# A hybrid decoder block: convolution's carry summed on GpSimd, gates' input sums in one stage, unread work dropped, stages in another order

## The chip, the cores and the metric

The kernel runs on one core of one Trainium2 chip, as one program. The time is in device microseconds (us) of that core; three runs of the kernel before gave 2437.46, 2438.08 and 2443.91 us, median 2438.08. The engines are called as in the profile: PE is TensorE (matmuls; PEld its weight loads), DVE VectorE, ACT ScalarE, POOL GpSimd, SP SyncE, which issues most DMAs. Each engine takes its instructions in the order in which they were given to it, and an instruction that waits holds those behind it.

## What is computed

One decoder block over 2048 tokens of width 1024, all in float32. A norm, then one projection for two groups of heads: four of a gated delta rule (GDN) with a causal convolution of width 4 over the tokens on q, k and v, and four of retention; their outputs go through gates, an output projection and a residual sum; then a second norm, an MLP with a convolution of width 3 and a gate, a residual sum and a last norm. Cut to what matters here:

```python
def reference(x, ...):
    n = _rms_norm(x, attn_norm_w)
    (gq, gk, gv, gg, ga, gb, rq, rk, rv, rg) = split(n @ w_in)
    mix = concat([_gated_deltanet(gq, gk, gv, gg, ga, gb, ...), _retention(rq, rk, rv, rg)])
    h = x + mix @ w_out
    h = h + _conv_glu_mlp(_rms_norm(h, mlp_norm_w), mlp_w_up, mlp_conv_w, mlp_w_down)
    return _rms_norm(h, final_norm_w)

# gated delta rule: q, k, v = silu(causal_conv4(.)); per chunk of tokens
t_mat = triangular_solve(eye + m, eye)          # m strictly lower, from k, beta and decay
def step(state, inp):                           # chunk after chunk
    u = u_b - w_c @ state
    o = qd_c @ state + qk_c @ u
    state = state * cd_c + kd_c.T @ u
    return state, o                             # first state: zeros; last state: not used
# retention: the same form, r = r * chunk_gamma + kv_c, first r: zeros, last r: not used
```

## The kernel before

**Tiling.** The tokens are cut into four blocks of 512 (NB = 4, TB = 512), a block into four chunks of 128 (NT = 4). Each float32 operand of a large matmul is split into a high and a low part (ScalarE copies the high part, VectorE subtracts), and each product is made as three matmul passes (`mm3`, lines 118 to 120; 539 to 541 for the token-major projections). The projections for the gates, the output projection (`W`) and both MLP products use a scheme with seven products in place of eight; their inputs are sums of quarters of the norm's output and of the weights. The MLP comes after the four blocks: `mlp_up` (line 1115) and `mlp_down` (line 1314).

**Stages.** `mixers` makes for each block a table of items: `pro` norm; `k0`, `q0`, `kq`, `v0` retention projections; `a`, `c`, `f`, `e`, `d` the GDN's projections with the convolution and what follows; `b0`, `b1` the triangular solve for the heads' first and second pair; `l0`, `l1` its upper levels; `r00` to `r13` the recurrence (pair, chunk); `h`, `y` retention; `g`, `G` gated outputs; `O`, `Q` weight sums for the seven-product schemes; `S` and `T` the sums of the norm's input for gate products 6, 7 and 5, 3; `P` and `p` gate products; `W` output projection; `N` second norm; `U` steps of MLP-up. The string `ORDER` lists the items of all blocks in the order in which they are written; the digit behind `U` says nothing, each takes the next step. From this a scheduler with a model of the engines' times makes the order of each engine's instructions, and buffers are given out from rings whose sizes are in `BUFS`.

**The convolution** (`conv`, line 404) works on a tile of 128 channels and 512 tokens: ScalarE scales the last tap, VectorE adds the shifted other taps (line 408). The first three tokens also need the three tokens before the block: `halo` keeps these, VectorE multiplies and adds them (line 412, 1, 2 and 3 columns) and copies the block's last three into it (line 414).

**The solve** (`gdn_base`, the part of `b0`, `b1`): its input goes through DRAM (written from ScalarE's queue, read into `Nb`, line 772), GpSimd makes 62 dependent steps (lines 781 and 783, alternating; the printed shape shrinks from 31 to 1 columns), the result is written to DRAM (line 786), read back as `AT` (line 794), and VectorE transposes it to `NT` (line 796).

**The recurrence** (`gdn_rec`, line 846), for a pair of heads and a chunk: TensorE `ks` (860, state times k and q), VectorE `kv` (863), TensorE `wps` (870), VectorE `u` (873, printed as `pers`), TensorE `sps` (878), VectorE state (880) and output (883). The next chunk's `ks` needs the state.

**Retention** (`ret_head`, `ret_out`): TensorE `rr` (964) makes each chunk's share of the state, `ro` (992, 993) the output from the chunk itself and from the state.

**Gates' sums** (`combos`, line 455): for each of two stages the four loads of `xT` (462), ScalarE's scaling (465), three or four VectorE sums (468), the split.

**The last norm** (`final`, line 1347): sum of the two halves' squares, scaling and epsilon (1350), power on GpSimd (1351), then the two halves of the output on ScalarE and VectorE.

## Time and profile before

| | |
|---|---|
| runs | 2437.46, 2438.08, 2443.91 us |
| profiled execution: span from first to last instruction | 2432.2 us |
| profiled execution: its own time beside the span | not listed; the median run is 5.9 us above the span |
| instructions | 35992 |
| TensorE busy | 2383.1 us (98%) |
| VectorE / ScalarE / GpSimd busy | 1658.6 / 1073.5 / 422.5 us |
| DMA | 652.40 MB, mean 268 GB/s |

In the rows a matmul's name is out<-in. `x2` behind a row of the timeline stands for instructions in a row of one kind; the bracket gives the engine's idle time before and what ended it. The stretches give for each engine the busy time within a part of the span, and the clock that was granted to TensorE as a share of full speed. A float32 matmul of 128x128 on 128x128 appears as two rows, a pass of the split products as one.

### The profile page before, as it was taken

Reading aid. Unit: us, or ns where it says so; the run is one execution under the profiler, and the core shown is the slowest. Engines: PE = TensorE matmul, PEld = TensorE weight load, DVE = VectorE, ACT = ScalarE, POOL = GpSimd, SP = SyncE. Lnnn points to the kernel's source line nnn. Section 1 sums busy time; section 2 is a strip of 40 time slices with the busy share of each in tenths; the row PEclk is TensorE's granted clock in tenths of the full one; section 3 lists DMA queues with packets and bytes.
Section 4 is the critical chain, followed back from the end, with each engine's and each line's share of the span. In section 5 each row is a group of like instructions: output and inputs, shape, how many; then the busy total and the mean of one; then the engine's idle time right before and its main releaser. Section 6 shows DMA issues by size and latency. Waiting matters only on the chain.

```text
span 2432.2 us, 35992 instructions
## 1 busy us (share of the span) xinstructions
PE 2383.1 (98%) x12404; PEld 2004.0 (82%) x12404; DVE 1658.6 (68%) x3187; ACT 1073.5 (44%) x2286; POOL 422.5 (17%) x753
## 2 busy tenths in 40 slices
PE   8999899999999999999999999999999999999998
PEld 8888788888887888887788888888888888888887
DVE  6965786574744872778889888995556676554684
ACT  6744555555444652466543434432222233432341
POOL 2154113510043003130000100000000002431030
PEclk9999999999999999999999999999999999999999
DMA  9955789986767874697898878767768588764782
GB/s 333 381 194 186 304 305 365 318 317 242 286 238 251 307 253 156 227 344 292 325 357 315 305 284 315 291 241 255 250 230 313 198 276 275 262 215 148 224 249 103
DMA packets 307142, 652.40 MB, mean 268 GB/s; under 512 B 51024, under 2 KB 130320, under 8 KB 306960
## 3 DMA queue, kind: packets, MB, share of 16 engines
q1 hardware_dynamic: 290240, 635.80, 73.8%
q10 hardware_dynamic: 16720, 14.30, 1.9%
q8 instruction: 98, 1.61, 0.3%
q14 instruction: 84, 0.69, 0.1%
HBM read 444.12 MB, written 205.88 MB: 267 GB/s over the span
## 4 chain that ended last, share of the span: by engine, by line
PE 52%; DVE 1%; issue 0%; ACT 0%; DMA 0%; POOLq 0%; POOL 0%; ACTq 0%
PE p L118 11%; PE p L120 11%; PE p L119 11%; PE d L120 6%; PE d L119 6%; PE d L118 6%; PE p L1215 1%; PE p L1214 1%; PE p L1213 1%; PE wo L118 0%; PE wo L120 0%; PE wo L119 0%; DMA wv<-kW 0%; DVE st L1146 0%; DVE x L1125 0%
## 5 line engine op out<-in xcount | busy, mean ns | idle before, releaser
L119 PE MATMUL p<-x,wu 128*128 128x512 f32 x1176 | 457.5, 389 | 0.7 <-DVE x L1125 0.5
L118 PE MATMUL p<-x,wu 128*128 128x512 f32 x1176 | 452.7, 389 | 0.0
L120 PE MATMUL p<-x,wu 128*128 128x512 f32 x1176 | 450.1, 389 | 0.0
L119 PEld LDWEIGHTS p<-x,wu 128*128 128x128 f32 x1176 | 220.8, 188 | 47.3 <-DVE x L1125 1.5
L118 PEld LDWEIGHTS p<-x,wu 128*128 128x128 f32 x1176 | 220.7, 188 | 46.0 <-ACT x L1124 0.3
L120 PEld LDWEIGHTS p<-x,wu 128*128 128x128 f32 x1176 | 220.7, 188 | 45.7
L1253 DVE SCALAR_TENSOR_TENSOR acc<-uc,base,acc 128x1022 f32<-128x1022 f32 (+1 forms) x176 | 220.8, 1278 | 37.4 <-ACT acc L1250 37.2
L1206 DVE TENSOR_TENSOR uc<-p,uc 128x512 f32<-128x512 f32 x224 | 153.0, 686 | 134.3 <-PE p L120 130.0
L539 PE MATMUL tok<-wc,n 128*128 128x512 f32 (+2 forms) x576 | 196.4, 351 | 7.7 <-ACT n L449 5.3
L540 PE MATMUL tok<-wc,n 128*128 128x512 f32 (+2 forms) x576 | 199.4, 348 | 0.0
L541 PE MATMUL tok<-wc,n 128*128 128x512 f32 (+2 forms) x576 | 195.9, 348 | 1.3 <-DVE n L452 1.3
L184 POOL TENSOR_TENSOR vt<-vr 128x512 f32<-128x512 f32 x44 | 71.9, 1634 | 639.0 <-DMA vr<-in_w_d 440.7
L118 PE MATMUL d<-v,uu 128*128 128x512 f32 x448 | 174.3, 389 | 0.0
L119 PE MATMUL d<-v,uu 128*128 128x512 f32 x448 | 174.3, 389 | 0.0
L120 PE MATMUL d<-v,uu 128*128 128x512 f32 x448 | 174.3, 389 | 0.0
L118 PE MATMUL chm<-n,wc 128*128 128x512 f32 x384 | 152.5, 397 | 1.8 <-ACT og L583 1.8
L119 PE MATMUL chm<-n,wc 128*128 128x512 f32 x384 | 151.6, 395 | 0.0
L120 PE MATMUL chm<-n,wc 128*128 128x512 f32 x384 | 151.3, 394 | 0.0
L1250 ACT ACTIVATE acc<-uc,base 128x1024 f32<-128x1024 f32 x88 | 97.1, 1144 | 92.9 <-DVE uc L1206 46.3
L539 PEld LDWEIGHTS tok<-wc,n 128*128 128x128 f32 x576 | 109.9, 192 | 21.1 <-ACT n L449 5.3
L408 DVE SCALAR_TENSOR_TENSOR ca<-ca,base 128x511 f32<-128x511 f32 (+2 forms) x144 | 109.5, 760 | 21.4 <-ACT ca L405 20.8
L540 PEld LDWEIGHTS tok<-wc,n 128*128 128x128 f32 x576 | 110.0, 191 | 12.3 <-DVE wc L208 0.2
(280 smaller groups left out, 5047.9 us busy)
## 6 DMA issues: line engine op xcount, KB each, us to landing
wu<-wu SPq DMA_DIRECT2D x308, 512.0 KB, 5.7
wc<-wd SPq DMA_DIRECT2D x116, 512.0 KB, 5.2
wv<-kW SPq DMA_DIRECT2D x112, 512.0 KB, 6.7
wc<-kP SPq DMA_DIRECT2D x84, 512.0 KB, 6.2
ur<-au SPq DMA_DIRECT2D x56, 512.0 KB, 5.1
wd<-wc SPq DMA_DIRECT2D x44, 512.0 KB, 7.3
wur<-in_w_u SPq DMA_DIRECT2D x44, 512.0 KB, 6.1
au<-st SPq DMA_DIRECT2D x88, 256.0 KB, 5.5
```

Of the source, the lines that this page charges most:

```text
L118: PE.matmul(ps, ah, bh, start=(first and i == 0), stop=False, skip_group_check=chk)
L119: PE.matmul(ps, ah, bl, start=False, stop=False, skip_group_check=chk)
L120: PE.matmul(ps, al, bh, start=False, stop=(i == n - 1), skip_group_check=chk)
L184: POOL.tensor_tensor(tt[:, j], a, b_, op=ALU.subtract)
L408: DVE.scalar_tensor_tensor(acc[:, s:], ps[:, :TB - s], w, acc[:, s:], op0=ALU.mult, op1=ALU.add)
L539: PE.matmul(ps, ah, wh, start=(k == 0), stop=False)
L540: PE.matmul(ps, ah, wl, start=False, stop=False)
L541: PE.matmul(ps, al_, wh, start=False, stop=(k == KT - 1))
L1206: add = lambda o, ps, a: DVE.tensor_tensor(o, ps, a, op=ALU.add)
L1213: PE.matmul(ps[i], wh, xh, start=(kt == 0), stop=False)
L1250: ACT.activation(acc, u, AF.Copy, scale=mcw[:, ci, 2:3])
L1253: DVE.scalar_tensor_tensor(acc[:, t:], u[:, :T2 - t], w, acc[:, t:], op0=ALU.mult, op1=ALU.add)
```

## The change

1. **Convolution.** What the next block needs of the last three tokens is multiplied and summed ahead, on GpSimd (three multiplications and two additions on 1 to 3 columns), not in the last block. In the next block VectorE adds the three columns in one instruction.
2. **Gates' sums.** `T` is gone; `S` makes the sums for products 6, 7, 5 and 3 from one load of each `xT` part and one scaling, with four sums instead of three and four.
3. **Unread work.** In the first chunk of block 0 the state is zero: `ks` and what reads it is left out there, the state is copied instead of updated, and the states are no longer set to zero. In the last chunk of block 3 the state's update is left out, with the scaled keys, `rr` and the retention state that only it needs.
4. **Last norm.** In the last output tile the second half's sum of squares is scaled at product 5, the first half's square is scaled as it is made, and one instruction between them and the power is gone.
5. **Order and buffers.** `ORDER` and some sizes in `BUFS` are new.

```diff
-BUFS = {... "NT": 6, "AT": 10, "o": 6, ... "wsq": 5, ... "sc": 15, ... "Nb": 6, ... "rrow": 5}
+BUFS = {... "NT": 8, "AT": 11, "o": 7, ... "wsq": 6, ... "sc": 14, ... "Nb": 7, ... "rrow": 4}
-ORDER = ("... 0r10 0r11 0p0 1pro 0O3 0h2 0Q0 0r12 0y2 0p1 0g0 1k0 0r13 0h3 ... 1S 1kq 1P1 1h2 1y2 1l1 1r03 1h3 1P4 1T 1P6 ..."
-         "... 3r11 3r12 3y3 2W4 2N 3g1 3W1 3r13 3W2 3G1 3W6 3W7 3W5 U1 U2 U3 U4 3W4 3W3 U9 U0 U6 U7 U8 U5 3N U10")
+ORDER = ("... 0r10 0r11 0r12 0p0 0p1 0O3 0h2 0Q0 0y2 0r13 1pro 0g0 0h3 1k0 ... 1S 1kq 1P1 1h2 1y2 1l1 1r03 1h3 1P4 1P6 ..."
+         "... 3r11 2W4 3y3 3r12 2N 3r13 3g1 3W1 U0 U9 3W2 3G1 3W6 U1 3W7 U2 U3 U4 3W5 U8 3W4 3W3 U6 U7 3N U10 U5")
...
-    for t in Sst + Rst:
-        POOL.memset(t, 0.0)
...
-        if not first:
-            for s in range(1, ntap):
-                w = wt[:, ntap - 1 - s:ntap - s]
-                DVE.scalar_tensor_tensor(acc[:, :s], halo[:, ntap - 1 - s:], w, acc[:, :s],
-                                         op0=ALU.mult, op1=ALU.add)
-        DVE.tensor_copy(halo, ps[:, TB - (ntap - 1):])
+            DVE.tensor_tensor(acc[:, :ntap - 1], acc[:, :ntap - 1], halo, op=ALU.add)
+        if not last:
+            POOL.tensor_scalar(halo, ps[:, TB - (ntap - 1):], wt[:, :1], None, op0=ALU.mult)
+            for s in range(1, ntap - 1):
+                tmp = small("ht", 2, 4)[:, :s]
+                POOL.tensor_scalar(tmp, ps[:, TB - s:], wt[:, ntap - 1 - s:ntap - s], None, op0=ALU.mult)
+                POOL.tensor_tensor(halo[:, :s], halo[:, :s], tmp, op=ALU.add)
...
-                    j = int(5 not in ids)
-                    tt(j, ALU.add, a21, a22)
-                    if 6 in ids:
-                        tt(0, ALU.subtract, tm[:, j], a11)
-                        tt(1, ALU.subtract, a11, a21)
-                    else:
-                        tt(1, ALU.subtract, a12, a22)
-                        tt(2, ALU.subtract, a11, a21)
-                        tt(1, ALU.add, tm[:, 1], tm[:, 2])
+                tt(1, ALU.subtract, a11, a21)
+                tt(2, ALU.add, a21, a22)
+                tt(0, ALU.subtract, tm[:, 2], a11)
+                tt(3, ALU.subtract, a12, tm[:, 0])
+                for j, ids in ((0, (6, 7)), (2, (5, 3))):
...
-                for c in range(NT):
+                for c in range(NT - (b == NB - 1)):
                     ACT.activation(kd[:, c * P:(c + 1) * P], ps[:, c * P:(c + 1) * P], AF.Copy,
...
+                fresh, ending = b == 0 and c == 0, b == NB - 1 and c == NT - 1
+                if not fresh:
+                    ps = rbank("ks")
...
+                        if k or not ending:
+                            PE.matmul(ps[:, (k * n + i) * P:(k * n + i + 1) * P], e[w][:, sl],
+                                      u[:, i * P:(i + 1) * P], start=True, stop=True)
...
+                    if fresh:
+                        DVE.tensor_copy(Sst[h], pn)
+                    elif not ending:
...
             if tp == 7:
+                ss = sst[t1][:, 1:]
+                DVE.tensor_scalar(ss, ss, 1.0 / D, EPS, op0=ALU.mult, op1=ALU.add)
                 DVE.tensor_tensor(c22, c22, fnw[:, TB:], op=ALU.mult)
...
-            square(t1, 0)
-            final(t1, n == len(steps) - 1)
+            last = n == len(steps) - 1
+            square(t1, 0, D ** -0.5 if last else 1.0)
+            final(t1, last)
```

**What moves, on VectorE, block 0's second pair.** Three places of the order follow. The first is VectorE around the transpose of block 0's second solve (`AT` to `NT`, line 796), where block 1's norm (`n1`) and its weights' split (`wc`) are being made; `kv` and `pers5` are the recurrence of the first pair. Before:

```order
L863 SCALAR_TENSOR_TENSOR kv_893<-ks_1825,pers4_547,kv_893 128x128
L863 SCALAR_TENSOR_TENSOR kv_1070<-ks_1825,pers4_547,kv_1070 128x128
L796 STREAM_TRANSPOSE NT_1286<-AT_1285 128x512
L452 SCALAR_TENSOR_TENSOR n1_2525<-xk_2520,base_60,n1_2525 128x512
L452 SCALAR_TENSOR_TENSOR n1_2530<-xk_2528,base_60,n1_2530 128x512
L356 TENSOR_TENSOR wc_2484<-wraw_2485,wc_2484 128x264
L356 TENSOR_TENSOR wc_2491<-wraw_2485,wc_2491 128x264
L796 STREAM_TRANSPOSE NT_1575<-AT_1574 128x512
L452 SCALAR_TENSOR_TENSOR n1_2533<-xk_2528,base_60,n1_2533 128x512
L356 TENSOR_TENSOR wc_2496<-wraw_2497,wc_2496 128x264
L873 TENSOR_TENSOR pers5_1309<-wps_1834,pers4_547 128x256
```

After (the same transpose is now line 790, the state's update 883, the output 889, a weight sum 295, the gated output 572, `kv` 859):

```order
L883 SCALAR_TENSOR_TENSOR pers2_124<-pers2_124,pers4_405,sps_1858 128x128 x2
L889 TENSOR_TENSOR o_1830<-sps_1858,o_1830 128x2x128
L452 SCALAR_TENSOR_TENSOR n1_2864<-xk_2862,base_60,n1_2864 128x512
L354 TENSOR_TENSOR wc_2534<-wraw_2528,wc_2534 128x264
L452 SCALAR_TENSOR_TENSOR n1_2867<-xk_2862,base_60,n1_2867 128x512
L902 SCALAR_TENSOR_TENSOR pers4_405<-pers4_405,pers5_1333 128x4
L295 TENSOR_TENSOR wg_2716<-wvt_2693,wg_2716 128x512
L572 SCALAR_TENSOR_TENSOR mix_2407<-o_1830,pers5_1333,mix_2407 128x128 x4
L295 TENSOR_TENSOR wg_2721<-wvt_2694,wg_2721 128x512
L790 STREAM_TRANSPOSE NT_1310<-AT_1309 128x512
L354 TENSOR_TENSOR wc_2539<-wraw_2540,wc_2539 128x264
L859 SCALAR_TENSOR_TENSOR kv_814<-ks_1881,pers4_405,kv_814 128x128
```

The transpose stood between `kv` and `pers5` of one chunk; now that chunk's state and output are made ahead of it.

**On GpSimd, block 2's first solve.** A row of the solve's two alternating steps (`Nb` is its input, `pers4` its result so far), before:

```order
L781 TENSOR_TENSOR pers4_547<-Nb_7557,pers4_547 128x3x22
L783 TENSOR_TENSOR pers4_547<-pers4_547 128x3x22
L781 TENSOR_TENSOR pers4_547<-Nb_7557,pers4_547 128x3x21
L783 TENSOR_TENSOR pers4_547<-pers4_547 128x3x21
L781 TENSOR_TENSOR pers4_547<-Nb_7557,pers4_547 128x3x20
L783 TENSOR_TENSOR pers4_547<-pers4_547 128x3x20
```

After (the steps are lines 775 and 777; lines 410 to 414 are the convolution's carry, `ca` its input):

```order
L775 TENSOR_TENSOR pers4_405<-Nb_7589,pers4_405 128x3x21
L410 TENSOR_SCALAR pers1_117<-ca_7521,base_60 128x3
L777 TENSOR_TENSOR pers4_405<-pers4_405 128x3x21
L414 TENSOR_TENSOR pers1_117<-pers1_117,pers3_225 128x1
L775 TENSOR_TENSOR pers4_405<-Nb_7589,pers4_405 128x3x20
L414 TENSOR_TENSOR pers1_117<-pers1_117,pers3_225 128x2
L777 TENSOR_TENSOR pers4_405<-pers4_405 128x3x20
```

The carry's steps stand within the solve; 15 of them in this solve.

**On TensorE, the last recurrence of block 3's second pair** (`ks`, `wps`, `sps` as above; `pers_1309` and `pers_1333` are `u`). Before:

```order
L870 MATMUL wps<-kv,AT 128x128 x2
L878 MATMUL sps<-pers_1309,kv 128x128 x2
L878 MATMUL sps<-pers_1309,AT 128x128 x2
L860 MATMUL ks<-pers_124,ykq 128x128 x4
L870 MATMUL wps<-kv,AT 128x128 x2
```

After (`p` are MLP-up products with their input `x` and weights `wu`, `nps` transposes of block 2's second norm):

```order
L856 MATMUL ks<-pers_124,ykq 128x128 x4
L118 MATMUL p_12346<-x_0_11939,wu 128x512
L119 MATMUL p_12346<-x_0_11939,wu 128x512
L120 MATMUL p_12346<-x_0_11939,wu 128x512
L1115 MATMUL nps<-base,Cw 128x128 x4
L867 MATMUL wps<-kv,AT 128x128 x2
L118 MATMUL p_12468<-x_0_11942,wu 128x512
L119 MATMUL p_12468<-x_0_11942,wu 128x512
L120 MATMUL p_12468<-x_0_11942,wu 128x512
L876 MATMUL sps<-pers_1333,kv 128x128 x2
```

Products of MLP-up and transposes now stand between the steps of one chunk.

More of the change, by code (lines that the diff above doesn't have):

```diff
@@ L955, in rstep @@
         def rstep(h, Rc, rr, c, dst):
+            if b == 0 and c == 0:
+                DVE.tensor_copy(dst, rr[:, :P])
+                return
             DVE.scalar_tensor_tensor(dst, Rc[c], float(gamma[h] ** 128), rr[:, c * P:(c + 1) * P], op0=ALU.mult, op1=ALU.add)
@@ L961, in f @@
                 rr = rbank("rr")
-                for c in range(NT):
+                for c in range(NT - (b == NB - 1)):
                     sl = slice(c * P, (c + 1) * P)
```

102 lines of the change are left out of this document (54 added, 48 removed), and 22 rows, old and new, of the table ORDER.

## The prediction

> **What bounds the kernel now.** I read the page's busy shares first, then the stretches of the span, then what TensorE waited for and the timelines around the long waits.
>
> ```profile
> span 2432.2 us, 35992 instructions
> PE 2383.1 (98%) x12404; PEld 2004.0 (82%) x12404; DVE 1658.6 (68%) x3187; ACT 1073.5 (44%) x2286; POOL 422.5 (17%) x753
> ```
>
> TensorE (PE) is busy for 98% of the span, so an engine that is only made less busy gives nothing. The time can fall in two ways: fewer matmuls, or fewer of the pauses of TensorE. This execution has a span of 2432.2 us; the three runs have a median of 2438.08, 5.9 us more. I make the sum against the span and add 5.9 at the end. The stretches (length, then busy time and count for each engine, granted clock, DMA share, GB/s) tell where the pauses are:
>
> ```profile
> core 0: us, PE busy (x) PEld busy (x) DVE busy (x) ACT busy (x) POOL busy (x), PEclk, DMA share, GB/s
> 0.00:180.00 180.00, 172.71 (x938) 148.18 (x939) 133.92 (x293) 110.49 (x281) 55.65 (x106) 1.00 0.82 303
> 180.00:300.00 120.00, 108.47 (x780) 94.31 (x779) 73.55 (x196) 61.98 (x155) 37.44 (x76) 0.96 0.68 243
> 520.00:540.00 20.00, 16.62 (x167) 13.50 (x166) 15.94 (x39) 10.88 (x20) 0.00 (x0) 0.83 0.84 323
> 720.00:800.00 80.00, 74.67 (x590) 62.90 (x589) 38.78 (x115) 36.55 (x104) 27.76 (x85) 1.00 0.77 259
> 1080.00:1130.00 50.00, 42.56 (x351) 36.64 (x350) 38.54 (x102) 36.23 (x95) 5.14 (x6) 0.97 0.69 244
> 1180.00:2416.00 1236.00, 1236.00 (x5470) 1023.84 (x5470) 878.47 (x1210) 448.50 (x659) 134.31 (x116) 1.00 0.75 260
> 2416.00:2432.20 16.20, 9.04 (x40) 7.13 (x38) 4.04 (x8) 2.17 (x5) 1.08 (x2) 0.91 0.17 65
> ```
>
> From 1180 to 2416 TensorE has no idle time at all and the full clock: there only fewer matmuls would help, and the change takes none away. The idle time is length less busy: 11.5 us where block 0's recurrence meets block 1's projections (180 to 300), 3.4 around 530, 5.3 at block 2's solve (720 to 800), 7.4 in the last recurrence (1080 to 1130). The clock adds to it: 0.96 of full speed over 120 us loses about 4.8 us, 0.97 over 50 us about 1.5.
>
> The largest pause is at 218 us:
>
> ```profile
> 209.54 0.61 DVE L863 SCALAR_TENSOR_TENSOR kv<-ks,pers,kv 128x128 f32<-128x128 f32 x2 [0.88 <-PE ks L860]
> 218.19 0.71 DVE L796 STREAM_TRANSPOSE NT<-AT 128x512 f32<-128x512 f32 x1 [8.04 <-DMA AT<-z]
> 222.40 0.42 DVE L873 TENSOR_TENSOR pers<-wps,pers 128x256 f32<-128x256 f32 x1
> ```
>
> ```profile
> 219.59 0.39 PE L541 MATMUL tok<-wc,n 128*128 128x264 f32 x1 [1.26 <-DVE n L452]
> 222.87 1.23 PE L878 MATMUL sps<-pers,kv 128*128 128x128 f32 x4 [2.89 <-DVE pers L873]
> ```
>
> ```profile
> 210.00:218.00 8.00, 8.00 (x43) 6.86 (x42) 0.15 (x1) 2.28 (x8) 1.92 (x3) 1.00 0.56 131
> 218.00:230.00 12.00, 7.84 (x69) 6.83 (x68) 10.07 (x22) 6.45 (x16) 1.02 (x1) 0.72 0.98 333
> 524.70:531.60 6.90, 5.71 (x70) 4.58 (x70) 5.90 (x15) 2.22 (x6) 0.00 (x0) 0.51 1.03 411
> ```
>
> VectorE (DVE) issues in order. It stands 8.04 us before a transpose whose input comes back from the solve through DRAM; queued behind it are the norm's `n`, the weights' `wc` and the recurrence's `pers`. TensorE lives for 8 us on what is ready (8.00 busy of 8.00) and then waits 1.26 for `n` and 2.89 for `pers`, 4.15 us together, and runs at 0.72 clock over the next 12 us. So half of VectorE's stall comes through to TensorE (4.15/8.04 = 0.52), and a slow clock follows.
>
> About that slow clock the Trainium skill ("TensorE: Matmul & The Clock Gate", section "What's actually happening") says that half speed comes after at least one idle window of about 3.4 us. The trace agrees only loosely: no idle row above is that long, 1.26 and 2.89 are apart, and the clock fell. By the rule any shorter pause is free of it, by the trace half a pause might not be: the sum below without the clock's 3.4 would be 2433.
>
> **The change, part by part.**
>
> *Matmuls dropped.* In the first chunk of block 0 the state is zero and in the last chunk of block 3 nobody reads the new state; 8 `ks`, 4 `sps`, 4 `rr` and 4 `ro` matmuls go. Each is two rows of the trace:
>
> ```profile
> L860 PE MATMUL ks<-pers,ykq 128*128 128x128 f32 x256 | 34.8, 276 | 0.7 <-DVE pers L880 0.6
> 1120.01 0.90 PE sps L878 x8
> ```
>
> The change issues 128 `ks` matmuls before and 120 after, against 256 rows: two each. The 276 ns is latency; in the chain of waits eight rows hold TensorE for 0.90 us, 0.1125 each. 20 x 2 x 0.1125 = **4.5 us less** (bounds: 0 where these matmuls stand beside a wait that stays, 34.8/256 = 0.136 each, 5.4, at most). Copies replace sums one for one. Eight memsets on GpSimd go from a start in which TensorE waits for loads: 0.
>
> *The end.* The last norm loses one step between the last square and the output:
>
> ```profile
> 2426.55 0.16 DVE L1349 TENSOR_TENSOR base<-base 128x1 f32<-128x1 f32 x1 [0.79 <-ACT jk L1364]
> 2426.75 0.15 DVE L1350 TENSOR_SCALAR base<-base 128x1 f32<-128x1 f32 x1
> 2426.98 0.54 POOL L1351 TENSOR_TENSOR base<-base 128x1 f32<-128x1 f32 x1 [6.94 <-DVE base L1350]
> ```
>
> From 2426.75 to 2426.98 goes: **0.2 us less**. The step that replaces it runs at product 5 of the down projection, under TensorE.
>
> *VectorE and ScalarE work.* Their rows (the first is a view by line, its times the lowest, the median and the highest in ns):
>
> ```profile
> L412 DVE SCALAR_TENSOR_TENSOR ca<-pers,base,ca x108: 204/215/305, 290.6 to 1021.8; 128x1 f32<-128x1 f32 x36, 128x2 f32<-128x2 f32 x36, 128x3 f32<-128x3 f32 x36
> L414 DVE COPY pers<-ca 128x3 f32<-128x3 f32 x48 | 9.3, 195 | 0.5
> L468 DVE TENSOR_TENSOR sm<-xk 128x256 f32<-128x256 f32 x60 | 23.9, 428 | 8.4 <-ACT xk L465 5.9 <-DMA n2d<-n2s 0.9 <-PE P L120 0.7
> L465 ACT ACTIVATE xk<-xk,base 128x512 f32<-128x512 f32 x48 | 31.7, 714 | 15.4 <-DMA xk<-in_xT 15.4
> ```
>
> The convolution's carry takes 108 x 0.215 + 9.3 = 32.5 us of VectorE; 36 additions at about 0.22 = 7.9 come back: 24.6 us less. The gates' input sums need 48 sums where 84 stood, 36 x 0.428 = 15.4 us less, 24 scalings less on ScalarE, 24 x 0.714 = 17.1, and 12 loads of `xT` less on SyncE's queue. All of it lies under TensorE, which is busy all through the stretches between the pauses; what it can shorten are the pauses, and none of the rows of the pauses names a carry, a sum or these loads as what is waited for. I put it at 0; a gain is bounded by the pauses in which VectorE is nearly full (38.54 of 50 us in the last recurrence, whose 7.4 idle are priced below). One thing moves forward: the sums for all four products are made in one stage, so the first product that reads them waits for four more conversions, at a place where TensorE has recurrence and projection work: 0 again, and some 2 us in each of three blocks where that work has run out (a sum and a scaling, 0.43 + 0.71, for each of the last two).
>
> *GpSimd work.* 36 convolutions hand on their carry, each by 5 instructions: 180 added, 8 memsets gone. No row of before has this operation on 128x1 to 128x3; the nearest are
>
> ```profile
> 724.29 0.22 POOL L781 TENSOR_TENSOR pers<-Nb,pers 128x16 f32<-128x16 f32 x1
> 724.59 0.23 POOL L783 TENSOR_TENSOR pers<-pers 128x16 f32<-128x16 f32 x1
> 130.85 0.63 POOL L781 TENSOR_TENSOR pers<-Nb,pers 128x54 f32<-128x54 f32 x1
> 184.17 0.28 POOL L781 TENSOR_TENSOR pers<-Nb,pers 128x54 f32<-128x54 f32 x1
> L1258 POOL COPY base<-uc 128x2 f32<-128x2 f32 x44 | 36.3, 826 | 389.3 <-DVE uc L1206 381.2 <-DVE pers L1053 8.0
> ```
>
> From one small start to the next it is 0.30 us; the tiny copy takes 0.826 on average, in a time in which VectorE is busier. So 0.30 to 0.83, 54 to 149 us in all, on an engine that is idle for 2000. I take 0.33, since most of the rows stand between solve steps like those at 724. Most of them cost nothing; those that count are queued inside a solve, because each delays the solve's end, and with it the DRAM trip, the transpose and everything behind that transpose. The order of the change puts 10 of them into the solve of block 0's first pair, 11 into that of block 1's first pair, 15 into that of block 2's first pair, none elsewhere. In block 0 the transpose after it is followed by much other work and is not in the list of pauses: 0 (0 to 3). In block 1 the order has some twenty more matmuls of 512 columns between the solve's input and its use, 20 x 1236/5470 = 4.5 us, against 11 x 0.33 = 3.6: 0. In block 2 nothing covers it:
>
> ```profile
> 698.97 0.24 POOL L781 TENSOR_TENSOR pers<-Nb,pers 128x31 f32<-128x31 f32 x1 [12.37 <-DMA Nb<-z]
> 725.18 0.22 POOL L783 TENSOR_TENSOR pers<-pers 128x8 f32<-128x8 f32 x1
> 733.63 0.71 DVE L796 STREAM_TRANSPOSE NT<-AT 128x512 f32<-128x512 f32 x1 [6.71 <-DMA AT<-z]
> 738.36 0.50 PE L539 MATMUL tok<-wc,n 128*128 128x512 f32 x1 [1.41 <-DVE AT L737]
> ```
>
> The solve takes 26.4 us, then VectorE already waits 6.71 us for the transpose's input and TensorE then 1.41. 15 x 0.33 = 5.0 us more lengthens a wait whose cover is used up: **5.0 us more** (bounds 0, if the scheduler has put the transpose later, and 15 x 0.83 = 12.4).
>
> *The new order, crossing of block 0 and block 1.* The first transpose of the second pair stands directly behind the `kv` of chunk 1 before; after, it stands behind chunk 1's state update and nine further rows, among them four weight sums, two norms and the gated outputs, 9 x 0.7 = 6.3 us of VectorE's work by the 0.71 of the 128x512 row. Nothing of chunk 1 is blocked by it any more. Against that two more GpSimd weight subtractions stand in the second solve:
>
> ```profile
> L288 POOL TENSOR_TENSOR wvt<-wvr,wvt 128x512 f32<-128x512 f32 x16 | 22.0, 1374 | 55.6 <-DMA wvr<-in_w_o 36.0 <-DMA wvr<-in_w_g 19.0 <-PE tok L541 0.3
> ```
>
> Its result is 2 x 1.374 = 2.7 later. Of the stall 8.0 - 6.3 + 2.7 = 4.4 remain. TensorE's 4.15 falls by half, 2.1, its slow clock (0.28 x 12 us = 3.4) goes, and of the other pauses to 300 some 1.5: **7 us less** (bounds: 0, the stall moves to chunk 2's `kv`; and 16.3, all of 11.5 idle and 4.8 of clock).
>
> *The new order, last recurrence.* Before, the last steps of the second pair follow each other with nothing between, after, MLP-up products stand between `ks`, `wps` and `sps`.
>
> ```profile
> 1108.07 1.19 PE L860 MATMUL ks<-pers,ykq 128*128 128x128 f32 x8 [0.56 <-DVE pers L880]
> 1110.82 0.68 PE L870 MATMUL wps<-kv,AT 128*128 128x128 f32 x4 [1.56 <-DVE kv L863]
> ```
>
> These two waits, 2.1 us, are covered by products of 0.7 each (three matmuls of 0.226); the others of the 7.4 stay, or come back where those products wait for their `x`: **2 us less** (bounds 0 and 8.9 with the clock).
>
> *Sum:* -4.5 - 0.2 + 5.0 - 7 - 2 = -8.7. 2432.2 - 8.7 = 2423.5, and with 5.9 about **2429 us**.
>
> **The rivals.**
>
> *The pauses only move.* An order written anew takes a stall from one place and puts it at another; the waits for transposes come from 62 dependent steps on GpSimd and two DRAM trips, and both are as long as before. Then only the matmuls and the end count: -4.7, 2433.4. For it, the list of VectorE's waits:
>
> ```profile
> DVE NT L796 <- DMA AT<-z: 24.5, 10, 8.0
> ```
>
> ten such stalls, and the change takes away none of what they wait for. Against it: TensorE feels only the long ones.
>
> *The crossing and the end close nearly whole.* The rows behind the transpose set free everything in the crossing, and MLP-up work fills the last recurrence; four fifths of 16.3 + 8.9 = 25.2 go, 20.2, and block 2's solve is hidden: -4.7 - 20.2 = -24.9, 2413. For it: these are waits for VectorE, which has 40 us less to do. Against it: the DRAM trip stays.
>
> *Slower: the carry steps hold up the solves.* GpSimd issues in order too. A carry step that waits for the convolution's input holds the solve behind it, and each step that runs beside VectorE's work is long: the same 128x54 step took 0.63 at 130.85 and 0.28 at 184.17. With 0.7 each the 36 steps inside solves make 25 us; at 0.52 of it through to TensorE that is 13.1, and two more stretches at half clock as at 524.7 (0.49 x 6.9 = 3.4 each) 6.8: -4.7 + 13.1 + 6.8 = +15.2, 2453. It decides from about 0.5 us per step: 36 x 0.5 x 0.52 = 9.4 and one slow stretch 3.4 are 12.8, and what the forecast gains is 4.7 + 7 + 2 = 13.7, of which the crossing's 7 would go too. For it: those rows, and the 0.826 of the tiny copy. Against it: three of eight solves only, and the solves near 184 and 724 show the low price.
>
> For the price the Trainium skill ("SBUF — State Buffer", section "Who interferes with whom") gives a cause: a VectorE instruction with two inputs in SBUF and a GpSimd one that reads SBUF exclude each other, and the later one blocks fully. By it the price depends on what VectorE does at that moment, and the carry steps also hold up VectorE. The 0.63 beside 0.28 agrees; no run here shows yet which it is for 128x3.
>
> **How the numbers follow.** Forecast, 2429: 0.48. Pauses only move, 2433: 0.22. Crossing and end close, 2413: 0.17. Slower, 2453: 0.13. A difference below 0.3%, 7.3 us, can hardly be told from none by a measurement like this one. The forecast's own range is 2421 to 2437 (7 and 5 us terms, each off by its half or its whole); it counts as faster in 8 of 12 and as no change otherwise, the moving pauses as no change in 7 of 10 and as faster in 2, the closing as faster, the slower case as slower. Faster: 0.32 + 0.04 + 0.17 = 0.53; slower: 0.13 + 0.02 = 0.15; no change: 0.32. For 8 in 10 the range takes in most of the closing case and the lower part of the slower one: 2412 to 2445.
>
> **What would show it.** Right: 40 fewer matmul rows; the transposes' longest wait in block 0 below 6 us and no `sps` wait of 2.9 behind it; idle time of TensorE from 180 to 300 near 7; GpSimd's solve in block 2's first pair about 31 us instead of 26.4; carry steps near 0.3; the idle time of the last recurrence near 5. Wrong: idle time from 180 to 300 unchanged or shifted into 300 to 540; carry steps of 0.6 and more, and solves over 36 us; new waits of TensorE for gate sums `sc`; idle time beyond 1180, where there was none.

## The result, and the profile after

The changed kernel has a median of 2443.67 us over 20 runs; the kernel before, run beside it on the same chips, has 2437.98 over 20. The ratio of runs is 1.0022, 95% from 1.0014 to 1.0030: 5.4 us slower (3.4 to 7.3), where 8.7 us less were forecast. It is inside the range and inside the 0.3% that I had called no change, but on the other side of zero. One of the 20 runs of after took 13680.53 us and is left out of the ratio. The profiled execution of after took 2443.99 us with a span of 2442.2, 10.0 more than the span of before. Not all of the 10.0 is the change: in after the time is 1.8 us above the span, so the profiled execution of before, with its span of 2432.2, was an estimated 4 us faster than before's median.

The first lines of after's page:

```profile
span 2442.2 us, 35882 instructions
PE 2387.2 (98%) x12364; PEld 2003.7 (82%) x12364; DVE 1630.4 (67%) x3017; ACT 1061.3 (43%) x2258; POOL 503.0 (21%) x925
```

The 40 matmul rows are gone (12404 to 12364), VectorE is busy for 28 us less (the prediction had reckoned 40), ScalarE for 12 less, GpSimd for 80 more. The engines did what the change says; the time did not follow. Where it went is read from the stretches. After's stretches, in the columns of the prediction (length, then busy time and count of PE, PEld, DVE, ACT, POOL; granted clock, DMA share, GB/s):

```profile
120.00:180.00 60.00, 55.08 (x355) 46.36 (x354) 36.17 (x85) 25.46 (x84) 33.36 (x81) 0.94 0.46 165
180.00:300.00 120.00, 110.53 (x712) 95.81 (x711) 77.69 (x196) 62.60 (x153) 46.72 (x88) 0.94 0.79 289
300.00:400.00 100.00, 95.05 (x495) 79.56 (x494) 71.66 (x151) 53.13 (x137) 29.20 (x43) 1.00 0.84 297
520.00:560.00 40.00, 39.53 (x364) 35.65 (x363) 27.01 (x81) 21.20 (x56) 3.46 (x3) 1.00 0.95 356
720.00:800.00 80.00, 72.51 (x567) 61.12 (x566) 38.08 (x110) 33.01 (x96) 30.97 (x96) 0.96 0.70 231
1030.00:1080.00 50.00, 45.69 (x342) 38.79 (x342) 29.33 (x77) 26.56 (x66) 23.08 (x66) 0.97 0.84 306
1080.00:1180.00 100.00, 93.76 (x544) 76.45 (x543) 85.44 (x176) 61.77 (x138) 8.16 (x8) 0.98 0.72 271
1180.00:2400.00 1220.00, 1217.78 (x5386) 1007.20 (x5385) 870.73 (x1204) 446.57 (x656) 129.14 (x111) 1.00 0.77 266
```

The same stretches of before, as far as the prediction doesn't show them:

```profile
120.00:180.00 60.00, 58.94 (x331) 49.29 (x330) 39.87 (x94) 28.05 (x90) 31.31 (x71) 1.00 0.55 192
300.00:400.00 100.00, 97.96 (x492) 81.94 (x491) 74.04 (x172) 52.80 (x147) 15.97 (x13) 0.99 0.89 328
520.00:560.00 40.00, 36.62 (x326) 33.06 (x325) 27.94 (x76) 23.45 (x55) 2.99 (x3) 0.91 0.80 303
1030.00:1080.00 50.00, 49.55 (x352) 42.47 (x351) 31.55 (x84) 26.91 (x69) 22.51 (x65) 1.00 0.97 354
1080.00:1180.00 100.00, 90.36 (x556) 74.71 (x555) 88.36 (x189) 61.18 (x139) 6.07 (x7) 0.98 0.82 298
1180.00:2400.00 1220.00, 1220.00 (x5400) 1010.57 (x5400) 872.96 (x1200) 446.64 (x654) 133.23 (x114) 1.00 0.76 263
```

A stretch loses its idle time (length less busy) and, at a lower clock, the missing share of its length. The clock is printed to two places, so a clock entry can be off by 0.3 us in a stretch of 60 and by 0.6 in one of 120. After against before, in us, from one execution of each:

| stretch | idle | clock | together |
|---|---|---|---|
| 120 to 180, block 0's first solve | +3.9 | +3.6 | +7.5 |
| 180 to 300, crossing of block 0 and 1 | -2.1 | +2.4 | +0.3 |
| 300 to 400 | +2.9 | -1.0 | +1.9 |
| 520 to 560 | -2.9 | -3.6 | -6.5 |
| 720 to 800, block 2's solves | +2.2 | +3.2 | +5.4 |
| 1030 to 1080, upper level of block 3's first pair | +3.9 | +1.5 | +5.4 |
| 1080 to 1180, last recurrence | -3.4 | 0 | -3.4 |
| 1180 to 2400 | +2.2 | 0 | +2.2 |

With +0.9 from the others these make about +13.7; 4.5 less for the matmuls dropped is +9.2, close to the +10.0 of the spans. That is more than the measured 5.4, and the table can't tell which of its rows hold the difference. The stretch that I had forecast to give most, the crossing, gave next to nothing: about as much as it lost in idle time came back as a slower clock. The largest single loss is at a place which the sum had at zero.

The longest waits of TensorE in after (time in all, times, longest), leaving out the one of 5.3 before its first matmul, then that at `sps`, and VectorE's for the solve's result:

```profile
PE yps L805 <- DVE pers L698: 4.5, 1, 4.5
PE yps L805 <- DVE NT L790: 3.5, 1, 3.5
PE ttps L832 <- DVE pers L828: 3.4, 1, 3.4
PE yps L805 <- ACT wc L353: 2.6, 1, 2.6
PE sps L876 <- DVE pers L870: 1.5, 3, 0.6
```

```profile
DVE NT L790 <- DMA AT<-z: 30.8, 9, 10.1
```

In before, the recurrence's `sps` led the list of these waits:

```profile
PE sps L878 <- DVE pers L873: 8.1, 7, 2.9
```

So the wait that the prediction named is gone (2.9 to 0.6 at most, 8.1 to 1.5 in all), and in its place TensorE waits before `yps`, the first matmul that reads the solve's result, and before `ttps`, a matmul of the solve's upper level. The name behind the arrow is the engine's event that came last by the profile; for the waits of 4.5 and 2.6 that event comes at most 0.15 us after the end of the transpose `NT`, and `NT` is what `yps` reads. VectorE's own wait for that result grew from 24.5 to 30.8 us, its longest from 8.0 to 10.1.

The place of the 4.5 and the 10.1, block 0's first solve, in after:

```profile
125.79 0.25 POOL L775 TENSOR_TENSOR pers<-Nb,pers 128x31 f32<-128x31 f32 x1
155.96 0.22 POOL L777 TENSOR_TENSOR pers<-pers 128x8 f32<-128x8 f32 x1
163.71 0.71 DVE L790 STREAM_TRANSPOSE NT<-AT 128x512 f32<-128x512 f32 x1 [10.08 <-DMA AT<-z]
164.57 0.64 PE L805 MATMUL yps<-NT 128*32 128x32 f32 x16 [4.51 <-DVE pers L698]
125.79:160.06 34.27, 34.27 (x183) 29.04 (x181) 16.45 (x31) 16.65 (x48) 27.07 (x75) 1.00 0.54 195
```

and in before, where the solve began at 128.32:

```profile
162.63 0.22 POOL L783 TENSOR_TENSOR pers<-pers 128x8 f32<-128x8 f32 x1
171.46 0.71 DVE L796 STREAM_TRANSPOSE NT<-AT 128x512 f32<-128x512 f32 x1 [0.30 <-DMA AT<-z]
172.30 0.45 PE L811 MATMUL yps<-NT 128*32 128x32 f32 x16
128.32:172.30 43.98, 43.98 (x236) 37.53 (x234) 25.89 (x60) 19.10 (x60) 27.31 (x68) 1.00 0.43 148
```

From the solve's first step to the matmul that reads its result the chain took 44.0 us before and 38.8 after: it is shorter, and it starts earlier. But before, TensorE's order held 44.0 us of other work between the two; after, it holds 34.3, and the difference to 38.8 is the wait of 4.5. A solve that is faster doesn't help if its cover (the other work that TensorE has meanwhile) shrinks by more.

The wait of 3.4 at `ttps` has another cause. In after, around it:

```profile
1037.98 2.62 ACT L464 ACTIVATE xk<-xk,base 128x512 f32<-128x512 f32 x4 [0.84 <-DMA xk<-in_xT]
1038.73 0.49 DVE L467 TENSOR_TENSOR sm<-xk 128x256 f32<-128x256 f32 x1 [6.98 <-ACT xk L464]
1044.21 1.08 PE L832 MATMUL ttps<-AT,pers 128*64 128x64 f32 x8 [3.44 <-DVE pers L828]
```

VectorE stands 6.98 us before the first of block 3's gate sums, until ScalarE has scaled the loaded `xT`, and the copies that the upper level needs (`pers`, line 828) are queued behind the sums. Over the span VectorE's waits for these scalings grew from 5.9 us (longest 2.1) to 13.9 (longest 7.0). Whether the merged sums or the new order put this wait there, no run parts.

### The profile page after: what moved, and what is told of

Same layout as the page of the kernel before. It is cut to its first block, busy times and chain, and to the rows that moved or that the text cites. A ratio compares the mean times of both kernels' runs of the same rounds, so it can differ in the third digit from the quotient of the medians.

```text
span 2442.2 us, 35882 instructions
## 1 busy us (share of the span) xinstructions
PE 2387.2 (98%) x12364; PEld 2003.7 (82%) x12364; DVE 1630.4 (67%) x3017; ACT 1061.3 (43%) x2258; POOL 503.0 (21%) x925
## 4 chain that ended last, share of the span: by engine, by line
PE 62%; POOL 3%; DMA 2%; issue 1%; DVE 1%; ACT 1%; SPq 0%; ACTq 0%; POOLq 0%; DVEq 0%
PE p L120 11%; PE p L118 11%; PE p L119 11%; PE d L120 6%; PE d L119 6%; PE d L118 6%; POOL pers L775 1%; POOL pers L777 1%; PE wo L118 1%; PE wo L120 1%; PE wo L119 1%; PE tok L533 1%; PE tok L534 1%; PE tok L535 1%; PE chm L119 1%
## 5 line engine op out<-in xcount | busy, mean ns | idle before, releaser
L406 DVE SCALAR_TENSOR_TENSOR ca<-ca,base 128x511 f32<-128x511 f32 (+2 forms) x144 | 111.9, 780 | 23.5 <-ACT ca L403 21.7
L534 PEld LDWEIGHTS tok<-wc,n 128*128 128x128 f32 x576 | 111.1, 193 | 12.3 <-DVE wc L354 0.2
```

What stands on the lines that cost most here:

```text
L406: DVE.scalar_tensor_tensor(acc[:, s:], ps[:, :TB - s], w, acc[:, s:], op0=ALU.mult, op1=ALU.add)
L534: PE.matmul(ps, ah, wl, start=False, stop=False)
```

## The experiments

The table lists all runs; each was timed beside the kernel before on the same chip, and ratios are to that. Since runs of different chips are compared, I compare ratios: a difference of 0.001 is 2.44 us, and its interval is the two intervals' half widths added as squares.

| run | median us | ratio to before | 95% |
|---|---|---|---|
| after | 2443.67 | 1.0022 | 1.0014 to 1.0030 |
| e1_carry_on_dve | 2472.10 | 1.0146 | 1.0132 to 1.0159 |
| e2_only_carry | 2479.19 | 1.0176 | 1.0162 to 1.0190 |
| e3_only_order | 2478.70 | 1.0173 | 1.0159 to 1.0187 |
| e4_old_order | 2469.03 | 1.0136 | 1.0120 to 1.0152 |
| e5_only_drop | 2476.04 | 1.0158 | 1.0143 to 1.0173 |
| e6_only_sums | 2451.97 | 1.0063 | 1.0048 to 1.0078 |
| n1_before_tie_pool | 2469.20 | 1.0145 | 1.0123 to 1.0167 |
| f0_old_rows | 2449.50 | 1.0048 | 1.0035 to 1.0060 |
| f1_drop_old_rows | 2445.30 | 1.0033 | 1.0021 to 1.0044 |
| f2_carry_old_rows | 2457.74 | 1.0076 | 1.0058 to 1.0095 |
| h1_transposes_later | 2449.57 | 1.0045 | 1.0028 to 1.0061 |
| f4_half_solves | 2433.34 | 0.9982 | 0.9973 to 0.9992 |
| g0_new_rows | 2462.65 | 1.0102 | 1.0088 to 1.0115 |
| g1_dvecarry_new_rows | 2457.46 | 1.0077 | 1.0060 to 1.0094 |
| g2_carry_behind | 2455.90 | 1.0077 | 1.0064 to 1.0091 |
| g3_carry_subs_behind | 2456.04 | 1.0075 | 1.0062 to 1.0088 |
| g4_half_solves_new | 2422.13 | 0.9941 | 0.9923 to 0.9959 |

### One part alone, the scheduler free

First I undid one part of the change, or made one alone, and let the scheduler order the engines anew.

e1: after, the carry back on VectorE.

```diff
-        if not last:
-            POOL.tensor_scalar(halo, ps[:, TB - (ntap - 1):], wt[:, :1], None, op0=ALU.mult)
...
+        DVE.tensor_copy(halo, ps[:, TB - (ntap - 1):])
```

> The changed kernel with the convolution's carry back on VectorE as before, all else as changed. Theory A (the carry's steps on GpSimd cost the time: they take 1 us and more in block 0 and stand ahead of and inside the solves): about 8 us less than the changed kernel, 2435 where before is 2438; the first solve starts when its input has landed, and the 4.5 us wait of TensorE behind its transpose is gone. Theory B (the new order puts the stalls at worse places, whoever sums the carry): within 3 us of the changed kernel, 2441 to 2446, and waits of 3 us and more behind transposes are still there.

e2: before, with the carry on GpSimd and nothing else of the change (the reverse of the diff above).

> The kernel before with the carry summed on GpSimd and nothing else changed (old order and buffers). Theory A: 5 to 10 us slower than before, carry steps near 1 us each in block 0, the first solve later by about 5 us. Theory B: within 3 us of before.

e3: before, with the new `ORDER` and `BUFS` alone; both old sum stages stand where the new order has `S`.

```diff
-ORDER = ("... 0r10 0r11 0p0 1pro 0O3 ...
+ORDER = ("... 0r10 0r11 0r12 0p0 0p1 0O3 ...
```

> The kernel before with the new order and the new buffer sizes alone; since the new order has no second stage for the gates' sums, both old stages are made one after the other at the place of the first. Theory A: no slower than before, down to 9 us faster, since the order without the carry on GpSimd is what was reckoned as a gain. Theory B: 5 to 12 us slower than before (the changed kernel is 5.4 slower though it has 4.7 us less work).

e4: after, with the old `ORDER` and `BUFS` (the reverse).

> The changed kernel with the old order and the old buffer sizes (the gates' sums stay in one stage, at the place of the first). Theory A: still slower than before by 3 us or more. Theory B: faster than before by 4 to 10 us, since the matmuls dropped are worth 4.5 and no stall was moved.

All four came out 1.4 to 1.8% slower, 33 to 43 us. The parts can't be read from that: taking the carry away from after costs 30 us, adding it to before costs 43. Two more parts alone, and a control that changes no work:

e5: before, with the unread work and the last norm's step dropped.

```diff
+                fresh, ending = b == 0 and c == 0, b == NB - 1 and c == NT - 1
+                if not fresh:
                     ps = rbank("ks")
```

> The kernel before with the unread work dropped and the last norm shortened, old order string and buffers, and the scheduler free. Parts with prices: 2432. Any order not picked with the code: 2455 to 2480, although 20 matmuls are gone.

e6: before, with the gates' sums made in one stage.

```diff
-        items.update({... "S": [(None, None, combos((6, 7)))], "T": [(None, None, combos((5, 3)))],
+        items.update({... "S": [(None, None, combos)], "T": [(None, None, lambda _: None)],
```

> The kernel before with the gates' input sums made in one stage, old order string and buffers, the scheduler free. Parts with prices: 2434 to 2440. Any order not picked with the code: 2455 to 2480.

n1: before, its work unchanged; GpSimd's instructions are tied to the order that they have in before anyway, and the scheduler is free with the other engines.

```diff
+                if _l is not None:
+                    tc.add_manual_dep(_ins[_p], _ins[_l].name, mybir.DependencyInfo(
+                        mybir.DependencyClass.NoSync, ...), reason="order")
```

> The code, the order string and the buffers of the kernel before; the only edit ties GpSimd's instructions to the order that they had anyway. It takes away and adds no work, but the scheduler makes another order of the other engines from it. If what the single parts of the change cost without their own order (32 to 42 us) is the price of the parts: within 5 us of before. If it is the price of any order that was not picked with the code: 20 to 45 us slower.

The control is 1.45% slower, 35 us, with the same work and the same order on GpSimd: what the tie shifted in the scheduler's account was enough for another order on the other engines. It is as large as e1 to e5 and larger than e6 (0.63%). In its trace GpSimd's 753 rows stand as in before, but 1473 of VectorE's 3187 places and 3181 of TensorE's 12404 hold another row. So none of the six differences can be put down to a part: each holds a new order of the engines too. e5 shows it best: 40 matmuls fewer, and 38 us slower.

### One part, all engines' orders held

Then I stored the order of each engine's instructions from before (or from after) and tied every engine to it, row for row, by dependencies that order and don't wait; I call such a kernel held. f0 is before, and g0 after, with nothing else. In g0, 48 copies and stores of the second norm on ScalarE were left untied, and 23 of ScalarE's rows there stand elsewhere than in after.

> The control: the kernel before with every engine's instructions tied to their old order and nothing else. The order is the same row for row; only the places of buffers and the waits that follow from them may differ. If the tie costs nothing: 2437, and the run with the dropped work (2445.3) shows a cost of dropping of 8. If the tie itself moves the time (buffers lie elsewhere, other waits): 2447 to 2452, and then dropping is worth about 4.5, the transposes later about 0, the carry on GpSimd about 8 more.

> The control on the other side: the changed kernel tied to its own order (but for the 48 copies and stores of the second norm on ScalarE). If the tie costs nothing: 2442 to 2446, and the carry back on VectorE in this order (2457.5) costs 14. If the tie costs as much as it may in the old order, 2452 to 2458: the carry's place is worth 0 to 5 in the new order.

The tie itself costs: f0 is 11.7 us above before, g0 19.5 (1.0102 less 1.0022) above after. But for these few the rows are the same; what differs, as far as I found, is where the buffers were laid in memory (a ring of four weight buffers instead of three in f0, three instead of two in g0). From here held kernels are compared with held kernels only.

**f1**, unread work and the last norm's step dropped, on before's rows (the diff of e5), and **f2**, the carry on GpSimd, on before's rows (the diff of e2, the new steps where the scheduler puts them: 5, 18 and 15 inside the first solves of blocks 0, 1 and 2, where the change has 10, 12 and 15):

> The kernel before with every engine's instructions held in the order that they had before (a list written into the kernel ties each instruction behind the one ahead of it on its engine), and only the unread work dropped and the last norm shortened. Theory A (each part has the price that its rows give, and what went wrong lies in the carry): 2437 - 4.7, so 2431 to 2434. Theory B (parts have no price of their own, any change of the stream costs tens of us): 2445 or more, although not one instruction has changed its place.

> The kernel before with the carry summed on GpSimd, all old instructions held in their old order; only the 180 new GpSimd rows take the place that the scheduler gives them. Theory A (the carry on GpSimd costs by its steps of up to 1 us ahead of and within solves): 3 to 10 us slower than before, solves 0, 2 and 4 end 4 to 7 us later. Theory C (the carry is nearly free, what cost 42 us in the run with the old order string was the rescheduling of everything else): within 3 us of before.

f1 against f0: -0.0015 ± 0.0017, -3.7 us (-7.8 to +0.5). f2 against f0: +0.0028 ± 0.0022, +6.8 us (1.4 to 12.3).

**g1**, after's rows with the carry on VectorE (the diff of e1):

> The changed kernel with the carry back on VectorE, all other instructions held in the order of the changed kernel (but for the 48 copies and stores of the second norm on ScalarE). Theory A: 5 to 10 us faster than the changed kernel, 2434 to 2438: the first solve starts 5 us earlier and is 5 us shorter, the 4.5 us wait of TensorE behind its transpose is gone. Theory C: within 3 us of the changed kernel, 2441 to 2446, so that the loss is the new order's.

g1 against g0: -0.0025 ± 0.0022, so the carry on GpSimd costs 6.1 us (0.7 to 11.4) on the new rows too. It is a loss in either order.

**g2**: after's rows, the 37 carry steps that stand inside solves (10, 12 and 15) moved on GpSimd's queue behind the solve; **g3**: the 8 weight subtractions inside solves as well.

```diff
 POOL, block 2's first pair
-  solve step 14; carry L413, L413; solve step 15; ... ; carry L414; solve step 61; solve step 62
+  solve step 14; solve step 15; ... ; solve step 61; solve step 62; carry L410; carry L413; ...
```

> The changed kernel's rows held in their order, with one move on GpSimd: the 37 carry steps that stand inside a solve (10, 12 and 15) stand behind its last step. Same work. Control: the new rows held, 2462.65; with the carry on VectorE 2457.46. If the carry costs by its place inside the solves: 2456 to 2459. If it costs by being on GpSimd ahead of the solves, or by what VectorE and GpSimd do to each other: 2461 to 2464.

> As before, and the weight subtractions on GpSimd that stand inside solves (4 of 1.3 us each in block 0's second and 4 in block 1's first) stand behind it too: these two solves end some 5 us earlier each. At the 0.17 us per us that halving the solves gave on the old rows, 2 to 3 us less than with the carry alone moved; at the 0.42 of the new rows, 4 to 5 us less. More than that if these solves are the ones that bind; no gain if the weights they delay are then what TensorE waits for.

g2 against g0: -0.0025 ± 0.0019, -6.1 us (-10.7 to -1.5): as much as taking the carry off GpSimd altogether (g2 against g1 0.0, within 5 us). The three solves are 3.4, 2.1 and 2.4 us shorter than in g0. So as far as these runs tell, the work on GpSimd is free, and its place within the solves is not. g3 is no faster than g2 (-0.0002), although two of its solves are 9.4 us shorter together: the subtractions inside cost nothing that can be seen, and not every solve counts.

**h1**: before's rows, but the two transposes of block 0's second solve stand on VectorE behind chunk 1's state update and output, as in the change.

```diff
 DVE
-  L863 kv (chunk 1); L796 transpose; ... ; L873 u; L880 state; L883 output
+  L863 kv (chunk 1); ... ; L873 u; L880 state; L883 output; L796 transpose x2
```

> The kernel before, every instruction in its old order but two: the two transposes behind block 0's second solve stand behind the state's update and the output of the recurrence's chunk 1 on VectorE, as the change has them, so nothing of chunk 1 waits for them. If the prediction's step on the crossing is right, the stall of 8.04 us falls below 4 and the time by 4 to 10 us. If the stall only moves to the next wait (the rival), the time stays within 3 us of before.

h1 against f0: -0.0003 ± 0.0021, -0.7 us (-5.8 to +4.4), medians 2449.57 and 2449.50. In f0 the stall before the first transpose was 4.76 us, not 8.04 as in before, and the `sps` wait 2.90, so there was less to gain; the interval still excludes -7. In h1's trace, TensorE around the place where before had its largest pause:

```profile
219.49 0.71 PE L878 MATMUL sps<-pers,kv 128*128 128x128 f32 x4 [0.85 <-DVE pers L873]
228.47 0.64 PE L811 MATMUL yps<-NT 128*32 128x32 f32 x16 [7.58 <-ACT pers L886]
```

and VectorE there:

```profile
227.29 0.42 DVE L883 TENSOR_TENSOR o<-sps,o 128x256 f32<-128x256 f32 x1
227.62 1.29 DVE L796 STREAM_TRANSPOSE NT<-AT 128x512 f32<-128x512 f32 x2
```

VectorE doesn't stall before the transposes any more and `sps` waits 0.85 us instead of 2.90. But the transposes now run some 9 us later after the solve's start, at 227.62, and TensorE, which has nothing left before `yps`, waits 7.58 us for the first of them. The pause moved and the time stayed.

**f4 and g4**: the rows of before and of after, with 240 of the 496 steps of the eight solves left out, 30 of 62 in each (every second step pair of a level), so the solve's result is another one; everything behind it runs as before. The stored orders are the same, less these rows.

```diff
-                for j in range(31):
+                for j in range(0, 31, 2):
```

> The old rows held in their order, with every second column step of the eight solves on GpSimd left out (31 of 62 rows each, so the result of the solve is not the reference's), about 12 us less in each solve. Its control is the kernel with the old rows held, 2449.5. The prediction took 0.52 us of TensorE for each us by which a solve ends later: by that a saving of at most 8 x 12 x 0.52 = 50, bounded by the pauses, so 20 or more. If the solves' ends are mostly covered by matmuls: 5 to 12 less.

> The rows of the changed kernel held in their order, with every second column step of the eight solves left out (30 of 62 rows each, as in the same run on the old rows; the solve's result is not the reference's). Its control is the kernel with the new rows held, 2462.65, which is 13.1 above the one with the old rows held although it has 4.2 us less of matmuls. If the new order loses by the solves' ends (less work of TensorE between a solve's input and its use): it falls by 25 to 35, to 2428 to 2437, next to the 2433.3 of the old rows. If the new order loses elsewhere (loads of weights, MLP-up's splits, the gates' sums): it falls by about 16, as the old rows did, to 2444 to 2449.

On before's rows this takes 16 us off (f4 - f0 = -0.0066 ± 0.0016, -12 to -20), on after's rows 39 (g4 - g0 = -0.0161 ± 0.0023, -34 to -45). By the traces the eight solves, each from its first step's start to its last step's end, went from 222.9 to 159.0 us together and from 227.1 to 151.3. Their steps are busy for 79 and 77 us less; the solves got shorter by 64 and 76, since GpSimd still waits for other rows that the held order keeps inside them. So on average of each us of solve 0.25 reaches the end in the old order, 0.52 in the new. With full solves the new rows are 13.2 us slower than the old (+0.0054 ± 0.0018), with half solves they are 10 us faster (-0.0041 ± 0.0021). In the stretches that had lost most, g0 with full solves,

```profile
120.00:180.00 60.00, 55.06 (x346) 46.27 (x346) 35.70 (x81) 27.30 (x91) 35.12 (x83) 0.94 0.50 180
720.00:800.00 80.00, 68.24 (x460) 56.64 (x459) 31.50 (x86) 27.85 (x77) 38.06 (x121) 0.97 0.64 210
1030.00:1080.00 50.00, 43.23 (x306) 35.39 (x305) 27.92 (x73) 21.18 (x46) 20.60 (x64) 0.97 0.75 272
PE yps L805 <- DVE NT L790: 10.0, 2, 6.4
PE yps L805 <- DVE pers L698: 4.6, 1, 4.6
```

and g4 with half of them, from the first to the last of the same matmuls, since g4 is ahead of g0 by up to 35 us there:

```profile
118.82:171.78 52.96, 52.96 (x346) 44.52 (x345) 35.39 (x81) 27.28 (x91) 23.29 (x53) 1.00 0.56 201
699.24:766.50 67.26, 66.08 (x460) 55.83 (x459) 30.98 (x84) 28.31 (x77) 21.71 (x65) 1.00 0.71 235
994.42:1039.76 45.34, 42.10 (x307) 35.64 (x305) 27.68 (x73) 21.10 (x46) 12.70 (x34) 0.96 0.83 298
PE yps L805 <- DVE NT L790: 1.1, 1, 1.1
```

TensorE is full at the full clock in the first, the idle time of the three falls from 23.5 to 4.4 us, and the waits at `yps` from 14.6 to 1.1. What is left in the third is a wait of 2.6 at `ttps`, which shorter solves don't take away. The new order is good for shorter solves; with the solves as long as they are, it uses their results too early.

**What stays open.** The held kernels differ from after in where the buffers lie, so g0's +13.2 against f0 isn't after's +5.4 against before. By difference, after's 5.4 is -3.7 for the dropped work, +6.1 for the carry and about +3.0 for all the rest: order, merged sums and ring sizes. With the three intervals together the 3.0 is uncertain by about 7 us, so it can't be told from zero. These three I couldn't part: a held order of before has no rows for merged sums. None of the kernels that do the whole work is faster than before.

## Why the prediction was wrong

*Matmuls dropped and the last norm, -4.7.* -3.7 measured, with an interval that holds both -4.7 and zero. Nothing speaks against the term.

*VectorE's and ScalarE's work, 0.* That less work there gives nothing is borne out as far as it was tried: with the carry on GpSimd, VectorE had less to do and the kernel got slower, not faster (f2, g0). What failed is that the merged gate sums were put at "0 again": at 1038 VectorE stands 6.98 us for their input, and TensorE 3.44 behind it.

*Carry steps, +5.0.* The size was about right (6.1 and 6.8), the grounds only in part. After's groups of these steps (busy time, mean ns):

```profile
L410 POOL TENSOR_SCALAR pers<-ca,base 128x3 f32<-128x3 f32 x36 | 23.2, 646 | 75.5 <-DVE ca L658 37.0 <-DVE ca L408 33.5 <-DVE pers L620 5.0
L413 POOL TENSOR_SCALAR pers<-ca,base 128x2 f32<-128x2 f32 x36 | 21.8, 604 | 0.0
L413 POOL TENSOR_SCALAR pers<-ca,base 128x1 f32<-128x1 f32 x36 | 20.2, 560 | 49.7 <-DVE ca L658 41.2 <-DVE pers L613 7.6 <-DVE pers L1065 0.6
```

With the additions' 22.5 us the 180 steps take 87.7, 0.49 each, where I had taken 0.33. I had charged block 2 alone, because block 0 and block 1 seemed covered; block 2's solve grew by only 2.0 us, to 28.4, although its 15 steps take 5.9. Block 1's first solve holds 12 steps in after, where I had counted 11. g2 shows that the price lies inside the solves, not in which of the three. So it was partly luck that the 5.0 came out right.

*The price of one step.* One group of them in block 0, on GpSimd in after:

```profile
74.52 1.25 POOL L410 TENSOR_SCALAR pers<-ca,base 128x3 f32<-128x3 f32 x1 [1.30 <-DVE ca L658]
75.75 1.97 POOL L413 TENSOR_SCALAR pers<-ca,base 128x1 f32<-128x1 f32 x2
77.69 0.46 POOL L414 TENSOR_TENSOR pers<-pers,pers 128x1 f32<-128x1 f32 x2
710.29 0.30 POOL L410 TENSOR_SCALAR pers<-ca,base 128x3 f32<-128x3 f32 x1
```

The same instruction takes 0.30 us at 710, where VectorE is busy for 4.75 of 8 us, and 1.25 at 74, where it is busy for 6.33 of 7; means above 0.55 come from such rows. By the Trainium skill ("SBUF — State Buffer", section "Who interferes with whom"), which the prediction cited, a VectorE instruction with two inputs in SBUF and a GpSimd one that reads SBUF exclude each other. That spread agrees with it; no run here changed VectorE's work alone to show it.

*Crossing, -7: the step that failed.* I followed VectorE's stall to the `sps` wait and took the transposes as free to go later, since "nothing of chunk 1 is blocked by it any more". That is so, and the `sps` wait did go. But I never asked what TensorE would do next without the transposes: `yps` needs them, and TensorE's own order had run out of other work. h1 made exactly this move and got about 0 (-5.8 to +4.4); in after the idle time there fell by 2.1 us and the slower clock took back about as much (2.4 by the printed clock). The slope of 0.52 us of TensorE per us of VectorE's stall came from one pause and was used as a property of the kernel; f4 and g4 give averages over eight solves, 0.25 per us of solve in the old order and 0.52 in the new, and that the second is the same figure is chance.

*Block 0's first solve, "0 (0 to 3)": the second step that failed.* I had looked at the list of pauses of before, in which this solve doesn't appear, and not at how much of TensorE's work the new order leaves between the solve and its reader. It left 34.3 us instead of 44.0, for a chain of 38.8: 4.5 us of wait, and 7.5 us lost with the clock. At block 2's solves (720 to 800, +5.4) part of the loss is of this kind, a wait of 3.5 at `yps` where before had 2.1; another 3.5 are waits for weights. No run gave the first solve its cover back on after's rows.

*Last recurrence, -2.* The idle time of 1080 to 1180 fell by 3.4, so the products between `ks` and `sps` cover about what I said, though a wait of 1.60 at `ks` is left; the 5.4 lost just before it have the other cause, the gate sums.

*The clock.* The prediction took the slow clock as something that goes with the pause. After has more of it, and not behind long pauses only:

```profile
224.41 0.28 PE L534 MATMUL tok<-wc,n 128*128 128x264 f32 x1
224.53 0.28 PE L535 MATMUL tok<-wc,n 128*128 128x264 f32 x1
227.44 0.38 PE L805 MATMUL yps<-NT 128*32 128x32 f32 x12 [2.63 <-ACT wc L353]
232.39 0.42 PE L533 MATMUL tok<-wc,n 128*128 128x264 f32 x1
232.61 0.42 PE L534 MATMUL tok<-wc,n 128*128 128x264 f32 x1
```

From one start to the next a matmul of 264 columns takes 0.12 us before the pause of 2.63 us and 0.22 after it. The Trainium skill ("TensorE: Matmul & The Clock Gate", section "What's actually happening") names an idle window of about 3.4 us before half speed. Here the wait of 2.63 was followed by half the rate, and waits of 1.60 (to 1111.78), 2.05 (to 442.71) and 2.24 (to 732.79) by some 3.3 us each at a clock of 0.50; where page and measurement differ, the measurement decides. In both traces, leaving out the end, the clock falls to 0.50 for stretches of about 3.4 or 6.8 us, five times in before and eight in after. By the table's sums, waits +6.3 and clock about +7, I estimate that a pause cost about twice its length here.

*The rivals.* "The pauses only move" has the right mechanism, shown by h1, and its 2433 is too low because they also grew. "The carry steps hold up the solves" has a real price, shown by g2, but 6 us and not the 20 that it was given (13.1 and 6.8). "The crossing closes" is out. Of the list of signs, idle time beyond 1180 came (+2.2); from 300 to 400 there is 2.9 more, but 2.9 less from 520 to 560. None of the signs was for a solve that loses its cover.

## What to carry to other kernels

When an order is written anew, take each long chain on a side engine (here 62 GpSimd steps and two DRAM trips) and measure two lengths: how long it takes from its input to the first reader, and how much of the bounding engine's other work the order puts between the two; the difference is the pause (38.8 less 34.3 is the 4.5 here), and moving the instruction that waits for the chain's result only picks which engine shows it. Small steps on a nearly idle in-order engine cost 6 us inside such chains here and nothing that could be seen behind them, so put them behind. To price one part of a change in a kernel whose order comes from a scheduler, hold all engines' orders and run a control that changes nothing; with the scheduler free, a control that changed no work moved the time by 35 us, as much as the parts did.

## What was not expected of the hardware

The same rows on every engine (in g0 all but those 23 of ScalarE), with buffers laid elsewhere in memory, took 11.7 us more (f0 against before, 8.5 to 14.6) and 19.5 us more (g0 against after). I had expected nothing. What of the layout does it, the one buffer more in a weight ring or the addresses, wasn't tried. And half of the solve's steps (77 and 79 us of GpSimd's busy time) were worth 16 us in one order and 39 in another, with the same work on TensorE.
